# One more convolution tap per pair of query tiles, low parts of the first query weights on VectorE, and a reordered tail in a one-core mixer block

## The chip, the cores and the metric

The kernel runs on one core of one Trainium2 chip. The metric is the device time of one execution in microseconds (us), and what is compared is the median over several executions. A core has TensorE (PE in the profile) for matrix products, with its weight loads shown apart (PEld), VectorE (DVE), ScalarE (ACT), GpSimd (POOL), and SyncE (SP), which here only issues DMA transfers.

## The reference, cut to what matters

One layer of a hybrid block on 1024 latent tokens of width 1024, with 256 context tokens, all in float32:

```
h  = rms_norm(x, g_pre) * (1 + sc) + sh            # sh, sc, gt from silu(c) @ w_mod
hc = rms_norm(ctx, g_pre) * (1 + scc) + shc
ua, gate_a, q, k, v, gate_b, gm = split(h @ w_in)   # 7680 columns
k_c, v_c from hc @ w_in
q, k = rope(rms_norm(q)), rope(rms_norm(k));  k_c = rms_norm(k_c)
o = softmax(q @ [k, k_c].T / 8) @ [v, v_c]          # 16 heads, 4 kv heads, head size 64
y_attn = (o * silu(gate_b)) @ w_attn_out
y = a * sigmoid(g)                                  # ua = [a, g]
y = depthwise_conv(y, 31 taps) + conv_b
y_conv = (silu(layer_norm(y)) * silu(gate_a)) @ w_conv_out
out = (sigmoid(ga) * y_conv + sigmoid(gb) * y_attn) @ w_out      # gm = [ga, gb]
x_new = x + gt * rms_norm(out, g_post)
```

## The kernel before, in words

**Products.** Every large product is made of three matmuls in a reduced format: each operand is split into a high part (a copy that rounds, mostly on ScalarE) and a low part (operand minus high part, on VectorE or GpSimd), and the product is high·high + low·high + high·low. A *filler* is one such triple of 128x512 for one of the projections that only need `h` or the convolution's output (`ppj<-t,whi`, `ppj<-t,wlo`): the program spreads the fillers through the other stages to keep TensorE fed, by `filler(n)` and, in the context part, by the numbers that the generators yield (`yield 4` means: four fillers before this generator goes on).

**The stages**, with the times they have in the profiled execution. From 0 to 60 us `x` is loaded, modulated and transposed. From 60 to 143 us comes the context: `ctx_h` normalises and transposes the context tokens, `ctx_kv` makes their keys and values, and `group_w(0)` loads and splits the weights `wgh`, `wgl` of keys, values and queries of group 0. From 143 to 523 us the 16 pairs of (group `g`, query pair `q`): each has 48 matmuls `po<-wgh/wgl`, then `per` fillers. In between, `pump(n)` lets VectorE do `n` convolution taps (`pconv<-y,cw,pconv`, one multiply-add over 128x1024, with the sum kept in PSUM), `qkv_rope` turns queries and keys, and `qkv_tr` transposes them on TensorE two fillers into the next pair. The number `per` is what is left of a fixed supply of fillers, divided by 16: 21 here. From 523 to 575 us the rest of the projections, and the taps in `conv_rest` (the sum in SBUF there, `acc<-y,cw,acc`). From 575 to 1218 us the attention: scores `ps`, exponentials `pe` on ScalarE, row maxima `mx` of `pm` on VectorE, sums `part` and `psum` on VectorE and GpSimd, a filler for each step, and beside it the generators of `later`, which each go on after as many steps as they yield: the rest of the taps, `z_prep` (layer norm and gate of the convolution), `left_operands` and `right_operands`. The last two make and store the operands of the tail.

**The tail**, from 1249 us, does the two products with `w_attn_out` (side 0) and `w_out` (side 1) by seven block products each instead of eight, as in Strassen's scheme: `STEPS` has 14 steps of 48 matmuls. One factor of a step is a weight block or a sum of two, the other a block of the data or a sum of two: `O4` holds the four blocks of side 0's data (from `heads_load`), `M4` those of side 1. `data_sum` makes sums of blocks on GpSimd (`t<-t,t`), `data_split` makes the parts `opd`, `coef_load(i)` brings the weights of step `i`: as finished parts (`W<-opD`, `whi`, `wlo`) where attention stored them (the lists `LEFT` and `RIGHT`), else raw (`RAW`: load `raw`, high part on ScalarE, low part on GpSimd). `merge` (tiles `t`, `y`, `acc`) adds the block products of side 0 into `M4`; `finish` adds those of side 1, normalises and stores the result.

**What sets the order.** From the context part to the end of the 16 pairs, VectorE, ScalarE and GpSimd run in the order in which the code is written; each engine takes its instructions strictly one after the other, so one that waits holds up all that stand behind it on its engine. In the attention and the tail a scheduler places them by readiness and priority, and `urgent()` raises the priority of what is written inside.

## Time and profile before

| | |
|---|---|
| runs | 1427.43, 1432.18, 1434.3 us; median 1432.18 |
| profiled execution | 1428.95 us, of which the profile's span is 1427.2 |
| TensorE busy | 1362.0 us, 95% of the span |
| VectorE busy | 1084.9 us, 76% |
| GpSimd busy | 725.7 us, 51% |
| ScalarE busy | 565.4 us, 40% |
| granted TensorE clock, mean | 0.983 of full speed |

A share is an average over the stages; which engine sets the pace is read stage by stage. A line of a timeline gives the start, the duration, the engine and the operation, and in brackets how long the engine sat idle before it and who released it. A line of waits gives who waited for whom: the sum, how often, and the longest. All instructions are recorded by one helper at line 51 (`L51`), so the tile names tell them apart. Runs of equal instructions are merged into one line with `xcount`.

### The profile page before, as it was taken

To read this page: it belongs to the slowest core of one execution; us is meant where nothing else is said; L and a number is where in the kernel's file an instruction comes from. 1 tells how busy PE (TensorE), PEld (TensorE's weight loads), DVE (VectorE), ACT (ScalarE), POOL (GpSimd) and SP (SyncE) were. 2 spreads that over 40 slices of the span, in tenths; PEclk is the share of its full clock that TensorE was granted. 3 is DMA by queue.
4 is the path that set the end of the run, shared out by engine and by line. 5 is a ranking of instruction groups with operands and counts; after the bars stand their busy time and mean duration, and the time that the engine had idled before them with its cause. 6 is when DMAs were issued, how large, how long until landed. Compare 5 with 4: busy or idle time off the path is not lost.

```text
span 1427.2 us, 19268 instructions
## 1 busy us (share of the span) xinstructions
PE 1362.0 (95%) x6520; PEld 1037.9 (73%) x6520; DVE 1084.9 (76%) x1351; ACT 565.4 (40%) x1388; POOL 725.7 (51%) x567
## 2 busy tenths in 40 slices
PE   5989899999999999989999999999999999999896
PEld 3766788898989887757666676666666666788684
DVE  3486888988899899997577576677587675468977
ACT  5542234344343431224344355445354344122232
POOL 1122537557656550246467655666457676243722
PEclk9999999999999999989999999999999999999997
DMA  9733424445434437413246434654265567598653
GB/s 323 259 126 96 142 89 142 159 154 163 153 119 141 157 117 218 140 52 107 72 156 207 133 119 138 173 170 132 84 200 177 196 212 235 196 324 288 225 162 132
DMA packets 149762, 235.05 MB, mean 165 GB/s; under 512 B 19184, under 2 KB 71964, under 8 KB 149664
## 3 DMA queue, kind: packets, MB, share of 16 engines
q1 hardware_dynamic: 138784, 214.89, 45.9%
q10 hardware_dynamic: 10880, 18.95, 4.5%
q8 instruction: 51, 0.84, 0.2%
q14 instruction: 47, 0.39, 0.1%
HBM read 156.22 MB, written 77.42 MB: 164 GB/s over the span
## 4 chain that ended last, share of the span: by engine, by line
PE 72%; DVE 12%; DMA 4%; issue 4%; POOL 3%; ACT 3%; SPq 1%; ACTq 0%; POOLq 0%; DVEq 0%
PE ppj L51 32%; PE po L51 19%; PE ps L51 12%; PE pm L51 9%; DVE acc L51 3%; DVE t L51 2%; DVE mx L51 1%; DVE pconv L51 1%; POOL wgl L51 1%; DMA W<-opD 1%; DVE y L51 1%; POOL wlo L51 1%; DVE ts L51 1%; DVE opd L51 1%; DMA wm<-in_wmod 1%
## 5 line engine op out<-in xcount | busy, mean ns | idle before, releaser
L51 PE MATMUL ppj<-t,whi 128*128 128x512 f32 x1728 | 612.2, 398 | 5.0 <-DVE t L51 2.6
L51 PEld LDWEIGHTS ppj<-t,whi 128*128 128x128 f32 x1728 | 326.3, 189 | 91.7 <-issue 19.4
L51 PE MATMUL ppj<-t,wlo 128*128 128x512 f32 x864 | 339.0, 392 | 1.7 <-POOL wlo L51 1.7
L51 DVE TENSOR_REDUCE mx<-pm 128x1 f32<-128x512 f32 (+1 forms) x320 | 213.6, 682 | 94.0 <-PE pm L51 91.6
L51 ACT ACTIVATE pe<-ps 128x512 f32<-128x512 f32 x320 | 189.9, 598 | 220.1 <-PE ps L51 182.6
L51 PE MATMUL ps<-r,kk 128*128 128x512 f32 (+1 forms) x640 | 202.0, 397 | 5.6 <-ACT pe L51 5.6
L51 DVE SCALAR_TENSOR_TENSOR pconv<-y,cw,pconv 128x1020 f32<-128x1020 f32 (+14 forms) x157 | 200.8, 1279 | 6.9 <-ACT pconv L51 3.2
L51 POOL TENSOR_TENSOR psum<-psum,pe 128x512 f32<-128x512 f32 x128 | 189.3, 1495 | 28.1 <-ACT pe L51 25.3
L51 PEld LDWEIGHTS ppj<-t,wlo 128*128 128x128 f32 x864 | 163.4, 189 | 31.7 <-POOL wlo L51 2.1
L51 POOL TENSOR_TENSOR psum<-psum,part 128x512 f32<-128x512 f32 x64 | 90.7, 1421 | 113.3 <-DVE part L51 109.1
L51 PEld LDWEIGHTS ps<-r,kk 128*128 128x128 f32 (+1 forms) x640 | 120.1, 189 | 36.7 <-ACT pe L51 9.9
L51 PE MATMUL po<-pe,vt 128*64 128x512 f32 x640 | 144.4, 597 | 0.0
L51 PE MATMUL pm<-kk,r 128*128 128x512 f32 (+1 forms) x384 | 128.5, 363 | 6.9 <-DVE mx L51 6.6
L51 PE MATMUL po<-wgh,t 128*128 128x384 f32 x512 | 132.0, 339 | 0.0
L51 POOL TENSOR_TENSOR wlo<-wraw,whi 128x512 fp32r<-128x512 f32 x61 | 84.9, 1398 | 80.9 <-ACT whi L51 61.5
L51 DVE SCALAR_TENSOR_TENSOR acc<-y,cw,acc 128x1017 f32<-128x1017 f32 (+14 forms) x77 | 114.3, 1496 | 0.7
L51 PEld LDWEIGHTS po<-pe,vt 128*64 128x64 f32 x640 | 43.1, 136 | 84.8 <-issue 84.4
L51 PEld LDWEIGHTS po<-wgh,t 128*128 128x128 f32 x512 | 94.6, 191 | 1.3
L51 PEld LDWEIGHTS pm<-kk,r 128*128 128x128 f32 x384 | 73.1, 191 | 26.1 <-DVE mx L51 9.5
L51 PE MATMUL po<-wgl,t 128*128 128x384 f32 x256 | 87.4, 341 | 4.2 <-POOL wgl L51 4.1
L51 ACT CAST whi<-wraw 128x512 fp32r<-128x512 f32 x114 | 70.2, 633 | 39.4 <-PE ppj L51 23.2
L51 POOL TENSOR_TENSOR psum<-pe,pe 128x512 f32<-128x512 f32 x32 | 43.7, 1368 | 79.0 <-ACT pe L51 77.5
(210 smaller groups left out, 1854.2 us busy)
## 6 DMA issues: line engine op xcount, KB each, us to landing
wraw<-in_wch SPq DMA_DIRECT2D x96, 256.0 KB
opD<-opw SPq DMA_DIRECT2D x56, 256.0 KB
wm<-in_wmod SPq DMA_DIRECT2D x24, 512.0 KB
W<-opD SPq DMA_DIRECT2D x48, 256.0 KB
r1D<-r1st SPq DMA_DIRECT2D x32, 256.0 KB
y<-accD SPq DMA_DIRECT2D x16, 512.0 KB
r<-r1D ACTq DMA_DIRECT2D x32, 256.0 KB
opD<-acc SPq DMA_DIRECT2D x10, 512.0 KB
```

Source lines behind the costliest of these rows:

```text
L51: i = f(*a, **k)
```

## The change

It has eight parts:

1. More fillers in the context part: `ctx_h` yields 4 and 5 instead of 3 and 4, the last weights of `ctx_kv` 4 instead of 2, its end 8 instead of 6, `group_w(0)` 10 instead of 6. These are 10 more, and `per` becomes 20 (16 fewer in the 16 pairs; six go behind them).
2. One more tap per pair, at `i == 10`: 12 instead of 11 in each of the 16 pairs.
3. The low parts `wgl` of group 0 on VectorE instead of GpSimd.
4. `left_operands` yields 2 instead of 4.
5. `right_operands` makes five right operands per row block instead of four: block (1, 0), raw weights of `w_out`, is split and stored in the attention, and the tail loads its parts instead of splitting it (`RAW` loses its first entry).
6. `z_prep` takes 15 steps per channel block instead of 11.
7. `heads_load` loads its blocks in the order 0, 2, 1, 3, and `coef_load(0)` comes behind the first of them.
8. `data_sum` and `data_split` become urgent; `data_sum(0, 4, 3, SUB, 0)` moves from within the steps to before them; the sums of side 1 are made one step earlier, with a sixth entry of `M4`.

```
-        yield 3                       # ctx_h
+        yield 4
         scale()
-        yield 4
+        yield 5
...
-            yield 2                   # ctx_kv, after each split of weights
+            yield 2 if raw is not raws[-1] else 4
...
-        yield 6                       # ctx_kv, before the keys are transposed
+        yield 8
...
-        yield 6                       # group_w
+        yield 6 if g else 10
...
-            split(hi[:], lo[:], raws[k // 2][:], le=G)
+            split(hi[:], lo[:], raws[k // 2][:], le=G if g else V)
...
-    RIGHT = ((5, 0, (1, SUB, 0)), (7, 1, (3, SUB, 1)), (6, 3, (3, SUB, 0)), (4, 2, (2, SUB, 3)))
-    RAW = {(1, 1): lambda t: wout[t * P:(t + 1) * P, 0:512],
-           (1, 2): lambda t: wout[(t + 4) * P:(t + 5) * P, 0:512],
+    RIGHT = ((1, 0, None), (5, 0, (1, SUB, 0)), (7, 1, (3, SUB, 1)), (6, 3, (3, SUB, 0)), (4, 2, (2, SUB, 3)))
+    RAW = {(1, 2): lambda t: wout[(t + 4) * P:(t + 5) * P, 0:512],
...
-                yield 4               # left_operands
+                yield 2
...
-            for n in range(-1, 6):    # right_operands
+            for n in range(7):
                 if 2 <= n:
                     SP.dma_start(out=opD[1][RIGHT[n - 2][0]][t][:], in_=f32(w[n - 2][:]))
-                if 1 <= n <= 4:
+                if 1 <= n <= 5:
                     i = RIGHT[n - 1][1]
                     V.tensor_tensor(out=w[n - 1][:, 1, :], in0=b[i], in1=f32(w[n - 1][:, 0, :]), op=SUB)
...
-                if 0 <= n < 4:
-                    w[n] = tl("acc", (P, 2, 512), 2, F32R) if (4 * t + n) % 3 else tl("ysum", (P, 2, 512), 1, F32R)
+                if n < 5:
+                    w[n] = tl("acc", (P, 2, 512), 2, F32R) if (5 * t + n) % 3 else tl("ysum", (P, 2, 512), 1, F32R)
                     S.copy(w[n][:, 0, :], b[RIGHT[n][1]])
...
-        for b in range(4):            # heads_load
-            if b == 3:
+        for b in (0, 2, 1, 3):
+            if b in (2, 3):
                 yield
...
-    DATA = (0, 2, 4, 0, 3, 1, 2, 0, 4, 0, 1, 3, 4, 2)
+    DATA = (0, 2, 4, 0, 3, 1, 2, 0, 4, 5, 1, 3, 4, 2)
...
-            G.tensor_tensor(out=blk[to][t][:], in0=blk[a][t][:], in1=blk[b][t][:], op=op)
+            with urgent():
+                G.tensor_tensor(out=blk[to][t][:], in0=blk[a][t][:], in1=blk[b][t][:], op=op)
...
-            split(hi[:], lo[:], blk[t][:], le=le)
+            with urgent():
+                split(hi[:], lo[:], blk[t][:], le=le)
...
-                if i % 5 in (1, 3):
+                if i % 5 in (1, 3) or i == 10:
                     pump(1)
...
+        if i == 4:
+            data_sum(1, 5, 0, SUB, 1)
         if i == 5:
-            data_sum(1, 0, 0, SUB, 1)
-            data_sum(1, 4, 3, SUB, 0)
+            data_sum(1, 4, 3, SUB, 5)
```

**Group 0's weights.** The low parts `wgl` feed the first pair's matmuls; `wlo` is the same for the filler weights, `y` and `ts` are results of fillers that VectorE takes out of PSUM, `acc` a tap. In the kernel before, GpSimd's queue at the end of the context part reads:

```order
L51 TENSOR_TENSOR wlo_1266<-wraw_1222,whi_1265 128x512
L51 TENSOR_TENSOR wgl_1373<-wgr_1334,wgh_1372 128x768
L51 TENSOR_TENSOR wlo_1383<-wraw_1360,whi_1382 128x512
L51 TENSOR_TENSOR wgl_1393<-wgr_1337,wgh_1392 128x768
L51 TENSOR_TENSOR wlo_1400<-wraw_1362,whi_1399 128x512
L51 TENSOR_TENSOR wgl_1416<-wgr_1340,wgh_1415 128x768
L51 TENSOR_TENSOR wgl_1433<-wgr_1343,wgh_1432 128x768
```

In the changed kernel GpSimd has only the `wlo` there, and VectorE's queue reads:

```order
L51 SCALAR_TENSOR_TENSOR y_382_1213<-ts_1214,ppj_1323 128x512
L51 SCALAR_TENSOR_TENSOR acc_898<-y_313_839,cw,acc_898 128x1020
L51 TENSOR_TENSOR wgl_1416<-wgr_1361,wgh_1415 128x768
L51 SCALAR_TENSOR_TENSOR y_382_1213<-ts_1273,ppj_1401 128x512
L51 SCALAR_TENSOR_TENSOR acc_898<-y_313_839,cw,acc_898 128x1019
L51 TENSOR_TENSOR wgl_1434<-wgr_1364,wgh_1433 128x768
L51 TENSOR_TENSOR wgl_1459<-wgr_1367,wgh_1458 128x768
L51 SCALAR_TENSOR_TENSOR acc_898<-y_313_839,cw,acc_898 128x1018
L51 SCALAR_TENSOR_TENSOR ts_1479<-ts_1479,ppj_1441 128x512
L51 TENSOR_TENSOR wgl_1484<-wgr_1370,wgh_1483 128x768
```

The four `wgl` left a queue where they alternated with the `wlo` of the fillers, for one where two taps and three results of fillers stand among them.

**The start of the attention.** VectorE's queue in the kernel before, at the second pair of sums `part`:

```order
L51 TENSOR_TENSOR part_6223<-pe_6190,pe_6221 128x512
L51 TENSOR_REDUCE mx_6146<-pm_6226 128x1
L51 SCALAR_TENSOR_TENSOR acc_5594<-y_1073_5043,cw,acc_5594 128x1013
L51 TENSOR_REDUCE mx_6146<-pm_6242 128x1
L51 TENSOR_REDUCE mx_6146<-pm_6253 128x1
L51 SCALAR_TENSOR_TENSOR acc_5594<-y_1073_5043,cw,acc_5594 128x1012
L51 TENSOR_TENSOR wlo_6407<-wraw_6355,whi_6406 128x512
L51 TENSOR_REDUCE mx_6146<-pm_6286 128x1
```

And in the changed kernel at the same place:

```order
L51 TENSOR_TENSOR part_6238<-pe_6198,pe_6236 128x512
L51 TENSOR_REDUCE mx_6155<-pm_6256 128x1
L51 TENSOR_REDUCE mx_6155<-pm_6267 128x1
L51 TENSOR_TENSOR wlo_6422<-wraw_6368,whi_6421 128x512
L51 TENSOR_REDUCE mx_6155<-pm_6299 128x1
```

Of the 240 taps 21 stand behind the first row maximum of the kernel before, 15 of them behind the first `part`; in the changed kernel 5 and none.

**The sums of side 1.** GpSimd's queue in the tail of the kernel before (`t` are the blocks of `M4`, the first line a low part of a raw weight block):

```order
L51 TENSOR_TENSOR wlo_12527<-wraw_12528,whi_12526 128x512
L51 TENSOR_TENSOR t_2938_12047<-t_2938_12047,t_3010_12343 128x512
L51 TENSOR_TENSOR t_3065_12558<-t_3038_12455,t_2938_12047 128x512
L51 TENSOR_TENSOR wlo_12533<-wraw_12534,whi_12532 128x512
L51 TENSOR_TENSOR t_3010_12343<-t_3010_12343,t_3038_12455 128x512
L51 TENSOR_TENSOR t_2940_12064<-t_2940_12064,t_3012_12360 128x512
```

And in the changed kernel, where the last low parts of side 0's data (`opd<-O,opd`) stand:

```order
L51 TENSOR_TENSOR opd_12439<-O_2855_11687,opd_12438 128x512
L51 TENSOR_TENSOR t_3037_12446<-t_2942_12063,t_3014_12359 128x512
L51 TENSOR_TENSOR t_3038_12448<-t_2944_12080,t_3016_12376 128x512
L51 TENSOR_TENSOR t_3039_12450<-t_2946_12097,t_3018_12393 128x512
L51 TENSOR_TENSOR opd_12443<-O_2856_11688,opd_12442 128x512
L51 TENSOR_TENSOR t_3040_12452<-t_2948_12114,t_3020_12410 128x512
```

The four `wlo` of raw weights are gone, and the first difference of side 1 has moved ahead of the last `opd` of side 0.

## Rows read from the trace of the kernel before

**Rows 1.** The page, busy time, its share of the span, and instructions of each engine.

```profile
PE 1362.0 (95%) x6520; PEld 1037.9 (73%) x6520; DVE 1084.9 (76%) x1351; ACT 565.4 (40%) x1388; POOL 725.7 (51%) x567
```

**Rows 2.** Waits of TensorE, by what it waited for: us in total, times, longest. The stretches, parted by "...", are 60 to 165, 523 to 575, 575 to 720, 1240 to 1300 and 1300 to 1428 us.

```profile
PE po L51 <- POOL wgl L51: 4.1, 2, 3.6
PE po L51 <- DVE x L51: 2.1, 2, 1.3
PE pm L51 <- DVE ts L51: 1.8, 1, 1.8
PE ppj L51 <- POOL wlo L51: 1.7, 1, 1.7
PE ps L51 <- DVE x L51: 1.7, 2, 1.4
...
PE ppj L51 <- DVE ts L51: 2.4, 2, 1.4
PE pm L51 <- DVE qk L51: 1.7, 1, 1.7
...
PE pm L51 <- DVE mx L51: 6.8, 5, 4.4
...
PE ps L51 <- DMA W<-opD: 1.7, 1, 1.7
...
PE ps L51 <- DVE opd L51: 4.9, 2, 4.3
PE pm L51 <- DVE opd L51: 2.9, 2, 2.7
```

**Rows 3.** Stretches of the span: its length, busy us (and instructions) of each engine, granted TensorE clock, DMA share, GB/s.

```profile
142.97:159.10 16.13, 12.05 (x51) 10.92 (x50) 15.92 (x11) 1.29 (x12) 9.15 (x4) 0.79 0.45 145
...
173.34:500.00 326.66, 326.52 (x1636) 289.85 (x1636) 288.56 (x328) 134.62 (x575) 187.04 (x197) 1.00 0.43 142
...
626.00:630.00 4.00, 3.28 (x9) 2.07 (x9) 4.00 (x6) 0.60 (x1) 0.31 (x1) 0.50 0.00 0
630.00:634.00 4.00, 4.00 (x11) 3.17 (x12) 4.00 (x6) 0.87 (x2) 0.00 (x0) 0.52 0.00 1
...
1342.00:1346.00 4.00, 3.36 (x7) 2.25 (x8) 4.00 (x4) 0.00 (x0) 3.38 (x3) 0.50 0.55 166
```

**Rows 4.** Timeline at the first pair, 137 to 155 us: start, duration, engine, operation, in brackets the idle time before it and its releaser; ScalarE, GpSimd and TensorE one after the other.

```profile
137.67 0.83 ACT L51 CAST wgh<-wgr 128x768 fp32r<-128x768 f32 x1 [7.08 <-DMA wgr<-in_wq]
...
138.58 1.85 POOL L51 TENSOR_TENSOR wgl<-wgr,wgh 128x768 fp32r<-128x768 f32 x1 [15.15 <-ACT wgh L51]
146.60 5.53 POOL L51 TENSOR_TENSOR wgl<-wgr,wgh 128x768 fp32r<-128x768 f32 x2
...
137.78 0.39 PE L51 MATMUL ppj<-t,wlo 128*128 128x512 f32 x1
138.46 0.39 PE L51 MATMUL ppj<-t,wlo 128*128 128x512 f32 x1
143.32 0.34 PE L51 MATMUL po<-wgl,t 128*128 128x384 f32 x1
143.86 0.34 PE L51 MATMUL po<-wgl,t 128*128 128x384 f32 x1
```

**Rows 5.** Groups of VectorE's instructions with shape, count, busy us and mean ns, and idle time before them: taps with the sum in PSUM (whole span), low parts of filler weights in 523 to 575 us.

```profile
L51 DVE SCALAR_TENSOR_TENSOR pconv<-y,cw,pconv 128x1020 f32<-128x1020 f32 (+14 forms) x157 | 200.8, 1279 | 6.9 <-ACT pconv L51 3.2
...
L51 DVE TENSOR_TENSOR wlo<-wraw,whi 128x512 fp32r<-128x512 f32 x7 | 4.8, 684 | 0.6 <-ACT whi L51 0.5
```

**Rows 6.** Waits of VectorE in 173.34 to 500 us (14 pairs): us in total, times, longest.

```profile
DVE ts L51 <- ACT ts L51: 9.1, 5, 2.9
DVE kst L51 <- ACT kst L51: 4.1, 3, 2.2
DVE y L51 <- PE ppj L51: 3.6, 2, 3.3
```

**Rows 7.** Timeline of one pair: the last step of the rope on VectorE, and TensorE's first transposes of what it made.

```profile
389.07 1.25 DVE L51 TENSOR_TENSOR qk<-qk,qkt 128x640 f32<-128x640 f32 x1
...
394.20 0.82 PE L51 MATMUL pm<-ident,qk 128*64 128x128 f32 x6
```

**Rows 8.** Timeline of VectorE at the start of the attention: four taps with the sum in SBUF, which stand ahead of a row maximum.

```profile
616.24 8.95 DVE L51 SCALAR_TENSOR_TENSOR acc<-y,cw,acc 128x1022 f32<-128x1022 f32 x4
```

**Rows 9.** Groups in the attention (720 to 1218 us): high parts of right operands on ScalarE, with the idle time before them and who ended it.

```profile
L51 ACT CAST acc<-y 128x512 fp32r<-128x512 f32 x10 | 6.2, 621 | 17.7 <-POOL y L51 10.9 <-DMA opD<-acc 6.8
```

**Rows 10.** Timeline of SP's issues before the tail.

```profile
1239.63 2.36 SPq L1125 DMA_DIRECT2D O<-ogD  x5
...
1243.07 4.19 SPq L1141 DMA_DIRECT2D W<-opD  x6
```

**Rows 11.** Timeline of the tail, 1309 to 1342 us: GpSimd, then VectorE.

```profile
1309.06 3.55 POOL L51 TENSOR_TENSOR wlo<-raw,whi 128x512 fp32r<-128x512 f32 x2
1322.55 18.78 POOL L51 TENSOR_TENSOR t<-t,t 128x512 f32<-128x512 f32 x11
...
1319.07 0.68 DVE L51 SCALAR_TENSOR_TENSOR t<-acc,t 128x512 f32<-128x512 f32 x1
1340.13 1.75 DVE L51 TENSOR_TENSOR opd<-t,opd 128x512 fp32r<-128x512 f32 x1
```

**Rows 12.** Waits of VectorE at the end, 1374 to 1427 us: us in total, times, longest.

```profile
DVE q L51 <- ACT junk L51: 3.7, 7, 0.9
```

More of the change, by code (lines that the diff above doesn't have):

```diff
@@ L637, in right_operands @@
             w = {}
-            for n in range(-1, 6):
+            for n in range(7):
                 if 2 <= n:
                     SP.dma_start(out=opD[1][RIGHT[n - 2][0]][t][:], in_=f32(w[n - 2][:]))
-                if 1 <= n <= 4:
+                if 1 <= n <= 5:
                     i = RIGHT[n - 1][1]
                     V.tensor_tensor(out=w[n - 1][:, 1, :], in0=b[i], in1=f32(w[n - 1][:, 0, :]), op=SUB)
-                if n + 1 < 4:
-                    i, (x, op, y) = RIGHT[n + 1][1:]
-                    G.tensor_tensor(out=b[i], in0=b[x], in1=b[y], op=op)
-                if 0 <= n < 4:
-                    w[n] = tl("acc", (P, 2, 512), 2, F32R) if (4 * t + n) % 3 else tl("ysum", (P, 2, 512), 1, F32R)
+                for j in {0: (), 1: (1, 2)}.get(n, (n + 1,)):
+                    if j < 5:
+                        i, (x, op, y) = RIGHT[j][1:]
+                        G.tensor_tensor(out=b[i], in0=b[x], in1=b[y], op=op)
+                if n < 5:
+                    w[n] = tl("acc", (P, 2, 512), 2, F32R) if (5 * t + n) % 3 else tl("ysum", (P, 2, 512), 1, F32R)
                     S.copy(w[n][:, 0, :], b[RIGHT[n][1]])
-                yield 2 if n >= 0 else 1
+                if n < 6:
+                    yield 2
     R1 = {}
@@ L1040, in z_prep @@
             SP.dma_start(out=g[:], in_=gaD[j][:])
-            yield 2
+            yield 3
             if j + 1 < KD:
                 load(j + 1)
-            yield 2
+            yield 3
             for tok in HALVES:
@@ L1047, in z_prep @@
                 yield 1
+            yield 1
             th = tl("ysum", (P, T), 1)
@@ L1051, in z_prep @@
             G.tensor_tensor(out=a[j][:], in0=a[j][:], in1=g[:], op=ALU.mult)
-            yield 2
+            yield 3
             for tok in HALVES:
@@ L1114, in block_kernel @@
     O4 = []
-    M4 = [[None] * 4 for _ in range(5)]
+    M4 = [[None] * 4 for _ in range(6)]
     data, coef, tmp, gates = {}, {}, {}, {}
@@ L1149, in data_sum @@
         for t in range(4):
-            if to == 4 != b:
-                blk[4][t] = tl("t2", (P, 512), 32)
-            G.tensor_tensor(out=blk[to][t][:], in0=blk[a][t][:], in1=blk[b][t][:], op=op)
+            if to > 3 and to != b:
+                blk[to][t] = tl("t2", (P, 512), 32)
+            with urgent():
+                G.tensor_tensor(out=blk[to][t][:], in0=blk[a][t][:], in1=blk[b][t][:], op=op)
     def data_split(i, le=V):
@@ L1158, in data_split @@
             hi, lo = tl("opd", (P, 512), 16, F32R, "C"), tl("opd", (P, 512), 16, F32R, "C")
-            split(hi[:], lo[:], blk[t][:], le=le)
+            with urgent():
+                split(hi[:], lo[:], blk[t][:], le=le)
             data[i].append((hi, lo))
     def data_ready(i):
-        if i == 2:
-            data_sum(0, 4, 3, SUB, 0)
         if i == 3:
@@ L1472, in block_kernel @@
     coef_load(0)
+    next(heads)
     filler(12)
@@ L1482, in block_kernel @@
     O4.append([None] * 4)
+    data_sum(0, 4, 3, SUB, 0)
     for t in range(4):
```

## The prediction

> **What bounds the kernel now.** I read the page first: TensorE is busy for 1362.0 of 1427.2 us [rows 1]. The change takes no matmul away, so all that it can win lies in the 65 us in which TensorE stands still, and in stretches where it works at half its clock. The second view is therefore TensorE's waits by stretch [rows 2]. The reader should see that they are few and each has an owner: 11.4 us up to the first pair of query tiles, 4.1 us behind the 16 pairs, 6.8 us at the start of the attention, 1.7 us before the tail, 7.8 us in it. The third view, busy time and clock by stretch [rows 3], shows two things. In the 14 pairs from 173 to 500 us TensorE is busy for 326.52 of 326.66 us: there is nothing to win in them. And after a wait of several us the granted clock is at 1.2 instead of 2.4 GHz for some us (0.50 and 0.52 of full speed from 626 to 634 us, 0.50 from 1342 to 1346 us), so that a long wait costs more than its own length.
>
> **Context and first pair.** A filler takes 138.46 − 137.78 = 0.68 us [rows 4]. Three matmuls `po` take 143.86 − 143.32 = 0.54 us, so the 48 of a pair take 16 x 0.54 = 8.6 us; the first pair's took about 16.1 us (51 matmuls in that stretch), at a mean clock of 0.79 [rows 3, 4]. The 7.5 us too much are the 4.1 us of waits for `wgl` [rows 2] and the clock behind them. The cause is GpSimd's queue: ScalarE's first `wgh` came late, after a wait of 7.08 us for its load, and from then GpSimd makes low parts of 1.85 us, at the end of 5.53/2 = 2.8 us each, with the `wlo` between them, until 146.60 + 5.53 = 152.1 us [rows 4]. The change gives four more fillers (2.7 us) between the loads and the first pair, and moves the four low parts to VectorE. The trace has no `wgl` there. The lower bound is 0.684 us for 128x512 with a quiet GpSimd [rows 5], times 768/512: 1.03 us. The upper is 1.75 us for 128x512 with a busy one [rows 11]: 2.6 us. I take the lower, since only the `wlo` are left on GpSimd. Four of 1.03, with the two taps (1.28 each [rows 5]) and three results of fillers (0.7 each) between them, are 8.8 us from 138.5 us on: until 147.3. TensorE comes to the pair at about 144 and to its last quarter 6.5 us later, at 150.5: covered by 3 us. At the upper price the last comes at 153.6, 3 us late, and with the clock behind it 6 us come back.
>
> At the four other waits one or two fillers more (0.7 to 1.4 us) stand ahead of what waits: 2.1 and 1.7 us for `x`, 1.8 us for `ts` [rows 2]; I count 1.4, 1.5 and 1.6. The 1.7 us for `wlo`, which stands behind a `wgl` in GpSimd's queue, go. With 7.5 that is 13.7; less some rest of waits, **−12** (bounds −6 and −14). The fillers themselves are moved, not added: 10 earlier and 6 later for 16 fewer in the pairs, which costs nothing where TensorE is the bound.
>
> **The 16 pairs.** A pair takes 326.66/14 = 23.33 us, and with one filler less 22.65. VectorE is busy for 288.56/14 = 20.61 us of it [rows 3]. Of its 38.1 idle us, 9.1 + 4.1 + 3.6 = 16.8 are waits for results that would lie ready if VectorE were late [rows 6]; the rest I count as part of its chain: (326.66 − 16.8)/14 = 22.13 us a pair. One more tap, 1.28 us [rows 5], makes 23.4: VectorE falls behind by 0.75 us a pair. It has a reserve: in the pair shown its rope ends at 389.07 + 1.25 = 390.3 us, and the first transposes of it start at 394.20 [rows 7]: 3.9 us, five pairs' worth. After that, by this bound, it sets the pace for eleven pairs: +8. By the other bound all its idle time can be filled (20.61 + 1.28 = 21.9 < 22.65): 0. I take +4, in the middle, since it is near neither. Behind the pairs stand 2.4 + 1.7 us of waits for `ts` and `qk` [rows 2], which the taps of the last pair cause; that pair has fewer taps now, but a later VectorE: I count −1. Together **+3** (bounds −3 and +8).
>
> **Start of the attention.** The 16 more taps before it leave 5 behind the first row maximum instead of 21, and none behind the first `part` instead of 15. Four of these took 8.95 us, 2.2 us each [rows 8], and the row maximum behind them gave the wait of 4.4 us among the 6.8 [rows 2]; from 626 to 634 us TensorE then worked at 1.2 GHz, which lost about 3.5 us more [rows 3]. That is 10.3; I take **−9** (bounds −6, if the scheduler puts the row maxima behind other work, and −10).
>
> **Attention.** Four more high parts on ScalarE (0.621 us each), which wait in its queue for GpSimd's sums and for stores, 17.7 us for ten [rows 9]; what is queued behind them are the exponentials, and TensorE's scores wait for those. `z_prep` is only spread. Bounds: 0, if they fall into ScalarE's idle time as most do now, and 4 x (0.6 + 1.8) = 10. I take **+1**, near the lower.
>
> **Tail.** The weights of step 0 stand behind eleven loads `O` in SP's queue (the last five and the weights: [rows 10]) and cost 1.7 us [rows 2]; with seven of those behind them: **−1.7**. The wait of 4.3 us for `opd` at 1342 us [rows 2] comes from VectorE's queue, which runs its three-tile work at 1.75 us a piece instead of 0.68 while GpSimd makes eleven sums in a row for 18.78 us [rows 11]. The change takes four `wlo` of 1.8 us off GpSimd [rows 11] and makes the first difference earlier, so the sums end some 7 us earlier and VectorE's last pieces run at the fast price. With the 0.6 us behind it and the half clock to 1346 us [rows 2, 3] the stall is worth 6.9 us; I take **−5.5** (bounds 0 and −7). The waits of 2.9 us at the end [rows 2] are worth less than they look, for there VectorE goes step by step with ScalarE (3.7 us of waits in seven pieces [rows 12]), and that chain ends the kernel: **−1** (bounds 0 and −3).
>
> By a rule of the Trainium skill (SBUF — State Buffer, section "Who interferes with whom"), a VectorE instruction with two SBUF inputs and a GpSimd instruction that reads SBUF shut each other out: the one that issues second waits for the whole of the first. The trace agrees in kind (0.68 and 1.75 us for pieces of one size, [rows 11]). By it the `wgl` on VectorE would pay the upper price whenever a `wlo` runs on GpSimd; the sum would be −19 instead of −25.
>
> **Sum.** −12 + 3 − 9 + 1 − 1.7 − 5.5 − 1 = −25.2 us. The profiled execution took 1428.95 us, so 1403.7 for one like it. It lies 3.2 us below the median of its runs, 1432.18; half of that I give to the median of the changed kernel, and round up: **1406 us**. The bounds of the terms together are −39 and +4; all ends on one side are unlikely.
>
> **Rivals.**
> - *The low parts on VectorE come late.* At 2.6 us a piece the first pair stalls again for 3 us, and with the clock 6 us come back: 1411–1412.
> - *VectorE becomes the bound in the pairs.* For it speaks the 23.4 against 22.65 us; against it the idle time that may be filled. It gives +8 in the pairs and another 4 to 5 us behind them, since VectorE then enters the rest of the taps late and the keys of the last pair with it: 1406 + 10 = 1416.
> - *The waits come back behind the next engine* in the attention and the tail: TensorE comes earlier to the next row maximum or part that is not ready. Then only the context and the first weights count, −12 + 3 + 1 − 1.7 = −9.7: 1421.
> - *Slower: ScalarE's queue in the attention.* Twenty high parts instead of sixteen share the same three buffers, and each must wait until its predecessor's store has landed; exponentials queue behind it. If each of the 20 holds TensorE for 2 us, with the clock behind every second one, that is 40 us and more: 1406 + 38 = 1444. It decides the sign from 25 us on, that is from 1.25 us for each of the twenty. Against it: the sixteen of now wait 1.8 us each on an engine that is busy for 40% [rows 1, 9].
>
> **How the numbers follow.** About 0.5%, 7 us, is what a measurement of this kernel can tell from no change: faster is below 1425, slower above 1439. The forecast has 0.47 (its own range 1397 to 1413), the late low parts 0.10, VectorE as the bound 0.17, the waits that come back 0.12, the slow attention 0.14. Of these, 0.02 of the third, 0.04 of the fourth and 0.04 of the fifth fall within 0.5%, 0.10 of the fifth beyond: faster 0.80, same 0.10, slower 0.10. The range 1395 to 1428 leaves out most of the fifth and what lies below the forecast.
>
> **What would show it.** Right: no wait for `wgl` and a first pair of about 8.6 us for its 48 matmuls; pairs of 22.65 us with TensorE busy throughout; no wait above 1 us for `mx` between 600 and 640 us (on the old time axis) and no half clock there; first matmuls of the tail without a wait for `W`; no 4 us wait for `opd` in side 1's first steps. Wrong: pairs longer than 22.8 us with TensorE waiting for `qk` (VectorE is the bound); TensorE waiting for `pe` by more than 10 us in the attention (ScalarE's queue); a granted clock of 0.5 where it is 1.00 now.

## The result: faster by a third of what was forecast

The changed kernel takes 1421.96 us (median of 10 runs, 1417.45 to 1426.28) against 1429.55 us for the kernel before (10 runs); the ratio is 0.9943, 95% interval 0.9924 to 0.9962. That is 8 us or 0.6% faster. The forecast was 1406 us, 26 us faster than the median then known; its range, 1395 to 1428, holds the result. The profiled execution of the changed kernel has a span of 1420.6 us against 1427.2.

TensorE's waits in the changed kernel (us in total, times, longest), which answer to [rows 2]. The stretches, parted by "...", are 60 to 165, 165 to 523, 523 to 575, 575 to 720, 720 to 1218, 1218 to 1300 and 1300 to 1428 us; sums of 0.5 us or less are left out:

```profile
PE ppj L51 <- DVE y L51: 3.2, 2, 3.0
PE pm L51 <- DMA wm<-in_wmod: 1.0, 2, 0.7
PE po L51 <- DVE x L51: 1.0, 1, 1.0
...
PE ppj L51 <- DVE ts L51: 3.4, 4, 1.5
PE pm L51 <- DVE qk L51: 2.9, 4, 2.0
PE ppj L51 <- DVE y L51: 2.0, 2, 1.3
...
PE ppj L51 <- DVE y L51: 1.9, 1, 1.9
PE ppj L51 <- DVE ts L51: 1.4, 2, 0.8
...
PE pm L51 <- DVE mx L51: 2.5, 3, 1.8
PE ppj L51 <- DVE ts L51: 1.3, 1, 1.3
...
PE ps L51 <- ACT pe L51: 6.4, 7, 1.5
...
PE pm L51 <- DMA whi<-opD: 2.1, 1, 2.1
...
PE ps L51 <- DVE opd L51: 0.9, 1, 0.9
```

The reader should see both halves. The waits that the prediction counted are gone or small: none for `wgl`, `wlo` and `W`, 2.5 us for `mx` instead of 6.8, 0.9 for `opd` instead of 7.8 in two lines. And there are new ones: 3.0 us for `y` in the context, 2.1 us for `whi` in the tail, and 8.3 us in the 16 pairs, where the kernel before had none.

The stretches show the same: the first pair's 48 matmuls (with three more), the 14 pairs behind it, and the start of the attention (columns as in [rows 3]).

```profile
149.10:157.80 8.70, 8.70 (x51) 8.64 (x50) 8.56 (x9) 1.38 (x13) 0.00 (x0) 1.00 0.73 221
171.14:502.50 331.36, 322.48 (x1597) 282.77 (x1597) 306.25 (x343) 134.64 (x580) 188.36 (x199) 0.99 0.44 141
604.30:676.10 71.80, 71.08 (x323) 48.82 (x323) 48.28 (x63) 32.32 (x57) 42.09 (x29) 1.00 0.27 86
```

The first pair takes 8.7 us instead of 16.1 and has its clock throughout; the 14 pairs, from which 14 fillers (9.5 us) were taken, take 331.4 us instead of 326.7; at the start of the attention TensorE is busy for 71.1 of 71.8 us.

**Where the time went.** Waits alone leave out what a low clock costs. So I took, for each stage, the time that it lasted less the number of TensorE's matmuls of each kind in it times their usual spacing in the kernel before. What is left I call lost time. It does not change when fillers move. In the attention its level means little, since the spacing there is itself set by other engines; only differences between kernels count. Executions of the same code differ by up to 4 us in the context and by about 3 us in other stages, so that smaller differences are no evidence by themselves. The first two rows of the table are best read as one: in the two other runs with the old code of this stretch (experiments 3 and 13) the context lost 2.5 and 3.8 us more than in the profile of the kernel before, and the first pair 2.7 and 2.8 us less. Together they came to −8.1 us where −12 was forecast.

```
us lost            before  after  change  forecast
context             33.4   32.8    -0.6     -4.5   (with the end of the first loads)
first pair           7.6    0.1    -7.5     -7.5
other 15 pairs       1.9   15.4   +13.5     +4
to the attention     7.1    9.4    +2.3     -1
start of attention  24.0   16.3    -7.7     -9
rest of attention  150.2  150.9    +0.7     +1
to the tail          6.8    5.0    -1.8     -1.7
tail, steps 0, 1     0.5    4.4    +3.9      0
tail, steps 7, 8     7.6    1.3    -6.3     -5.5
tail, steps 9 to 13  6.8    0.0    -6.9  }  -1
behind the matmuls  11.1   14.9    +3.8  }
sum                                -6.6
```

Five of the stages came as forecast or nearly; the 16 pairs, the stretch behind them, the context and a new wait in the tail's second step took the rest back.

### The profile page after: what moved, and what is told of

Its sections match the earlier page's. It is cut to its first block, busy times and chain, and to the rows that moved or that the text cites. A ratio compares the mean times of both kernels' runs of the same rounds, so it can differ in the third digit from the quotient of the medians.

```text
span 1420.6 us, 19284 instructions
## 1 busy us (share of the span) xinstructions
PE 1359.5 (96%) x6520; PEld 1033.5 (73%) x6520; DVE 1072.7 (76%) x1359; ACT 565.0 (40%) x1388; POOL 705.2 (50%) x559
## 4 chain that ended last, share of the span: by engine, by line
PE 55%; DVE 20%; issue 10%; DMA 5%; POOL 5%; ACT 3%; SPq 1%; ACTq 0%; POOLq 0%; DVEq 0%
PE ppj L51 21%; PE po L51 15%; PE ps L51 11%; PE pm L51 8%; DVE pconv L51 7%; DVE acc L51 2%; DVE t L51 2%; DVE qk L51 2%; POOL wlo L51 1%; DVE qkt L51 1%; DVE r1st L51 1%; DVE ts L51 1%; DVE y L51 1%; DMA wraw<-in_wch 1%; POOL y L51 1%
## 5 line engine op out<-in xcount | busy, mean ns | idle before, releaser
L51 PE MATMUL ppj<-t,whi 128*128 128x512 f32 x1728 | 617.0, 399 | 16.1 <-DVE y L51 7.0
L51 DVE SCALAR_TENSOR_TENSOR pconv<-y,cw,pconv 128x1012 f32<-128x1012 f32 (+14 forms) x174 | 222.5, 1279 | 10.0 <-ACT pconv L51 5.7
L51 POOL TENSOR_TENSOR psum<-psum,pe 128x512 f32<-128x512 f32 x128 | 184.8, 1458 | 27.7 <-ACT pe L51 24.3
L51 PEld LDWEIGHTS ps<-r,kk 128*128 128x128 f32 (+1 forms) x640 | 120.0, 189 | 38.5 <-ACT pe L51 11.8
L51 DVE SCALAR_TENSOR_TENSOR acc<-y,cw,acc 128x1009 f32<-128x1009 f32 (+14 forms) x60 | 80.3, 1339 | 2.3 <-ACT acc L51 1.3
```

Source lines behind the costliest of these rows:

```text
L51: i = f(*a, **k)
```

## The experiments

Each edit is against the changed kernel unless it says otherwise; the kernel before had medians of 1427.9 to 1429.5 us beside them. Ratios are to it; the changed kernel's is 0.9943.

**1. The extra tap undone.** (`z_prep` has its old yields, without which it does not end in time.)

```
-                if i % 5 in (1, 3) or i == 10:
+                if i % 5 in (1, 3):
```

> The changed kernel without its extra tap in the 16 pairs (11 taps each again) and with z_prep's old yields, which it then needs to end in time; all else as changed. My theory: the extra tap is what makes VectorE the bound in the pairs. Then TensorE's waits from 165 to 523 us fall from 9.0 to under 2 us and the lost time there by 12 us; in return the row maxima at the start of the attention wait again (6.8 us and half clock behind them, 8 us): about 1418 us against 1422 for the changed kernel. Rival: the pairs are slow because they are one filler shorter and GpSimd's left operands, made faster now, slow VectorE down; then the waits in the pairs stay above 5 us and the whole takes about 1429 us.

Measured: 1430.6 us, ratio 1.0009 (0.9995 to 1.0023). The waits of TensorE in the pairs:

```profile
PE pm L51 <- DVE qk L51: 1.8, 2, 1.3
PE ppj L51 <- DVE ts L51: 1.1, 1, 1.1
PE ppj L51 <- DVE y L51: 0.3, 1, 0.3
PE ppj L51 <- ACT ts L51: 0.3, 1, 0.3
```

The pairs lost 6.9 us instead of 15.4: the tap costs them 8.5, as my theory had it in kind, but 5 us of loss remain over the kernel before. What is left to explain them is the shorter pair (20 fillers) with the new yields of `left_operands` that go with it: this generator runs in the pairs, one step behind each filler (its `opw` are made from 175 to 528 us in the changed kernel), not in the attention as the description of the stages says. The time is not what the theory gave: the start of the attention lost 5.1 us more, the rest of it 7.5 more and the stage ahead 4.0. So the 16 taps are dearer behind the pairs than in them, by more than the first wait of the attention that I had priced; how much of the 7.5 us belongs to the old yields of `z_prep` is not shown.

**2. The extra tap in half of the pairs.**

```
+                if i % 5 in (1, 3) or i == 10 and q % 2:
```

> The changed kernel with the extra tap in every second pair only (8 more instead of 16). My theory, from VectorE's work per pair: 22.13 + 0.64 = 22.8 us against 22.65 of TensorE, so that it falls behind by 1 us over all pairs, within its reserve: waits of TensorE in the pairs below 3 us instead of 9.0, and 13 taps behind the first row maximum, few of them behind the first part: about 1412 us. Rival (each tap costs the same wherever it stands): the waits in the pairs halve, to 4 to 5 us, and half of the 8 us at the start of the attention come back: 1420 us.

Measured: 1424.73 us, ratio 0.9968 (0.9952 to 0.9984). The pairs lost 11.5 us, between 6.9 and 15.4, as the rival said: the cost goes with the number of taps, there is no reserve within which a few are free. The stage behind the pairs lost 16.5 us instead of 9.4; the code makes there, in one go, what is left of a channel's taps, and how many those are depends on the count before. That this is the cause was not shown.

**3. The extra tap alone, in the kernel before** (21 fillers per pair).

```
-                if i % 5 in (1, 3):
+                if i % 5 in (1, 3) or i == 10:
```

> The kernel before with the extra tap per pair alone. By my theory the pairs, at 23.33 us, lose less than 4 us, and the start of the attention gains the 8 us that it gained in the changed kernel: about 1424 us against 1429 before. By the rival (the tap makes VectorE the bound at 23.33 us too) the pairs lose 10 us or more and the time is 1431 us or above.

Measured: 1433.11 us, ratio 1.0024 (1.0005 to 1.0042): slower than before. The theory falls: with a pair of 23.33 us the pairs lost 11.8 us against 1.9. The start of the attention won 8.2 us, as in the changed kernel, and the stage ahead of it lost 5.5. TensorE's waits in 165 to 523 us, and the stretch of the pairs:

```profile
PE ppj L51 <- POOL wlo L51: 2.3, 1, 2.3
PE po L51 <- ACT qk L51: 1.8, 1, 1.8
PE ppj L51 <- DVE y L51: 1.7, 2, 1.1
PE pm L51 <- DVE qk L51: 0.5, 1, 0.5
```

```profile
172.90:510.20 337.30, 330.86 (x1640) 291.08 (x1639) 304.52 (x342) 133.93 (x575) 187.51 (x197) 0.99 0.42 138
```

VectorE is busy for 304.5 of 337.3 us, 90%; over the whole stretch it isn't full. And only 2.2 of the 6.3 us of waits are for VectorE itself. Before the wait for `wlo`, GpSimd had made a sum `ysum` of 2.40 us at 230.87 us, which in the kernel before came at 241.64 us, behind that `wlo`: one more tap per pair also shifts the end of each channel of the convolution, and with it work of other engines. That this shift makes the wait was not tested apart.

**4. 21 fillers again, the rest as changed** (the old yields in the context part and in `left_operands`).

```
-        yield 6 if g else 10
+        yield 6
...
-                yield 2
+                yield 4
```

> The changed kernel with the old yields of the context part and of left_operands, so that a pair has 21 fillers again; the extra tap, the low parts on VectorE and the tail as changed. My theory now: TensorE can't bear a VectorE that is late by 1.5 us, since it waits for results of fillers that VectorE takes out of PSUM in the order of its queue; a pair of 22.65 us is too short for VectorE with 11 or 12 taps, one of 23.33 us holds both. Then the lost time in the pairs falls from 15 to under 4 us, the waits for x and ts in the context come back (5 us), the first pair stays without a wait for wgl: about 1414 us. Rival: twelve taps (23.4 us by the prediction's bound) are too many at 23.33 us too; then 10 us are lost in the pairs and the whole takes 1421 us.

Measured: 1424.58 us, ratio 0.9959 (0.9944 to 0.9974). The pairs lost 10.3 us instead of 15.4, the context 3.9 more, the stage ahead of the attention 5.0 more; in sum the same. The rival was right: twelve taps are too many for 23.33 us too, and the shorter pair, with the yields of `left_operands`, costs 5 us more. In the context the waits for `x` and `ts` are back (5.6 us), but the wait for `y` at its end did not go with the added fillers; it is longer, in 60 to 165 us:

```profile
PE ppj L51 <- DVE y L51: 5.8, 1, 5.8
```

**5. to 7. The same tap at other places.** VectorE's work per pair is that of the changed kernel in all three: the extra tap leaves its place behind filler 11 for one of these.

```
-            pump(3)                                        # among the matmuls po
+            pump(4)
...
-                if i % 5 in (1, 3) or i == 10:
+                if i % 5 in (1, 3) or i == 4:              # behind the fifth filler
...
+                if i % 5 in (1, 3) or i == per - 1:        # behind the last filler
```

> The changed kernel with the extra tap of a pair moved: from between fillers 10 and 11 into the matmuls po of the pair, where three taps stand already and no filler's result waits for VectorE. VectorE's work per pair is the same. Theory (latency: what TensorE waits for are results of fillers that stand behind taps in VectorE's queue): the lost time in the pairs falls from 15 us to 11 or less, and the whole is 4 us faster than the changed kernel. Rival (VectorE's sum of work per pair decides): the lost time in the pairs stays at 13 to 17 us, the time at 1422 us.

> The changed kernel with the extra tap behind the fifth filler of a pair. In the trace of before VectorE's idle time lies in the middle of a pair (fillers 2 to 8). Theory (place): the lost time in the pairs falls below 12 us. Rival (any tap ahead of filler 10 delays the results behind it, as among the matmuls po, where 24 us were lost): more than 15 us are lost, the time is 1425 us or above.

> The changed kernel with the extra tap of a pair behind its last filler instead of behind the eleventh. The same work of VectorE per pair. Theory (place: a tap costs what it delays; in the changed kernel VectorE's queue is full from filler 10 on, and TensorE waits there, while behind the last filler come 8 us of matmuls po without a filler's result): lost time in the pairs 8 us or less against 15, the whole about 1415 us. Rival: the delay only moves to the rope, which stands next in VectorE's queue, and to the transposes that wait for it: lost time of 15 us or more, waits for qk instead of ts, 1422 us or above.

Measured: among the matmuls 1431.86 us (ratio 1.0020, 1.0004 to 1.0037), behind the fifth filler 1432.53 (1.0022, 1.0007 to 1.0038), behind the last 1426.09 (0.9979, 0.9966 to 0.9991). The pairs lost 23.9, 22.3 and 19.7 us, against 15.4 with the tap behind filler 11. The largest waits in 165 to 523 us, first with the tap among the matmuls, then behind the last filler:

```profile
PE ppj L51 <- DVE ts L51: 7.6, 5, 2.7
PE ppj L51 <- DVE y L51: 4.4, 2, 2.6
PE ppj L51 <- ACT ts L51: 3.1, 3, 1.2
PE pm L51 <- DVE qk L51: 0.9, 2, 0.7
```

```profile
PE pm L51 <- DVE qk L51: 7.7, 5, 2.7
PE ppj L51 <- DVE ts L51: 2.9, 2, 1.5
PE ppj L51 <- DVE y L51: 2.7, 2, 1.5
```

The work is the same and the loss differs by 8.5 us, so VectorE's sum per pair does not decide alone. The owner of the wait follows the tap: put ahead of the fillers, it delays their results (`ts`, `y`); put at the end, it delays the rope (`qk`); behind the fifth filler it delays both (7.2 us for `ts` and `y`, 4.8 for `qk`). But no place was free, and my guess at a better one was wrong three times: the changed kernel has the best of the four.

**8. Loads of group 0's weights earlier.**

```
-        yield 8                # end of ctx_kv
+        yield 6
...
-        yield 6 if g else 10   # group_w
+        yield 6 if g else 12
```

> The changed kernel with two of the fillers moved from before to behind the loads of group 0's weights (the end of ctx_kv yields 6 as before, group_w(0) 12). My theory: the wait of 3.0 us for y at 141 us and the half clock behind it come from those loads, which stand in SP's queue behind two loads of filler weights that wait for GpSimd; ScalarE's first wgh waits 10.2 us for them, VectorE's first wgl for that, and y stands behind it. Then the wait shrinks below 1 us and the time falls by 4 to 5 us, to about 1417 us. Rival: the loads of filler weights only move behind it and the wait goes to wlo or wgl at the first pair: 1422 us.

Measured: 1423.89 us, ratio 0.9955 (0.9938 to 0.9973): no gain. The wait for `y` fell from 3.0 to 2.1 us, a new one of 0.7 us for `ts` came, and the tail's second step lost 1.5 us more. Nothing of 4 us shows in the sum. The two loads of filler weights still stand ahead of those of group 0 in this run (issued at 132.23 and 135.80 us), so it did not take away what it was aimed at.

**9. The first low part back on GpSimd.**

```
-            split(hi[:], lo[:], raws[k // 2][:], le=G if g else V)
+            split(hi[:], lo[:], raws[k // 2][:], le=V if g == 0 and k else G)
```

> The changed kernel with the first of group 0's four low parts back on GpSimd, the other three on VectorE. Theory (the wait of 3.0 us for y at 141 us is y standing behind that low part in VectorE's queue, which waits for ScalarE's wgh and that for its load): the wait for y and the half clock behind it go, 4 to 5 us, with no new wait for wgl: 1417 us. Rival: a wait of the same size for wgl, wlo or ts follows within the next 10 us: 1422 us.

Measured: 1422.06 us, ratio 0.9950 (0.9931 to 0.9970): as the rival said. The chain at the end of the context in the changed kernel is this (ScalarE, GpSimd, VectorE, TensorE, then SP's issues):

```profile
142.18 0.83 ACT L51 CAST wgh<-wgr 128x768 fp32r<-128x768 f32 x1 [10.24 <-DMA wgr<-in_wq]
...
131.49 4.71 POOL L51 TENSOR_TENSOR wlo<-wraw,whi 128x512 fp32r<-128x512 f32 x2 [8.46 <-ACT whi L51]
145.36 3.53 POOL L51 TENSOR_TENSOR wlo<-wraw,whi 128x512 fp32r<-128x512 f32 x2 [9.15 <-ACT whi L51]
...
143.05 0.96 DVE L51 TENSOR_TENSOR wgl<-wgr,wgh 128x768 fp32r<-128x768 f32 x1 [5.76 <-ACT wgh L51]
143.92 0.68 DVE L51 SCALAR_TENSOR_TENSOR y<-ts,ppj 128x512 f32<-128x512 f32 x1
145.71 3.99 DVE L51 TENSOR_TENSOR wgl<-wgr,wgh 128x768 fp32r<-128x768 f32 x2
...
144.66 0.50 PE L51 MATMUL ppj<-t,whi 128*128 128x512 f32 x1 [3.02 <-DVE y L51]
...
134.01 2.55 SPq L146 DMA_DIRECT2D wraw<-in_wch  x2
137.57 0.42 SPq L581 DMA_DIRECT2D wgr<-in_wkv  x1
```

TensorE waits for `y`, which stands behind `wgl` in VectorE's queue; that waits for ScalarE's `wgh`, that for its load, and the load stood in SP's queue behind two loads of filler weights, which wait for GpSimd's `wlo`. Those two loads are not what makes the wait: in experiment 4 they don't stand there, and `y` waits 5.8 us. With the first `wgl` on GpSimd the `y` is free (0.2 us), and TensorE comes to the first pair 4.6 us earlier (144.5 instead of 149.1 us), where the weights are still missing:

```profile
PE po L51 <- DVE wgl L51: 2.8, 2, 2.4
PE po L51 <- DVE x L51: 1.0, 1, 1.0
PE po L51 <- POOL wgl L51: 0.9, 1, 0.9
```

The first pair then loses 6.2 us instead of 0.1, the context 4.8 less.

**10. and 11. The loads before the tail.** The changed kernel's old order of the heads' loads, and, apart from it, urgent loads for step 1.

```
-        for b in (0, 2, 1, 3):
-            if b in (2, 3):
+        for b in range(4):
+            if b == 3:
```

```
-    coef_load(1)
+    with urgent():
+        coef_load(1)
```

> The changed kernel with the old order of the heads' loads. If the order only moved a wait from step 0 (1.8 us for W) to step 1 (3.9 us for whi with the clock behind it), the old order is faster by 2 us: 1420 us. If the wait for whi has another cause (more loads in the tail), W waits again on top of it: 1424 us.

> The changed kernel with the loads of step 1's weights (whi, wlo) made urgent. My theory: the wait of 2.1 us for whi at 1259 us and the half clock behind it (3.9 us in all) come from the twelve loads of O that now stand in SP's queue between W and whi; with whi ahead of them the time falls by 3 to 4 us, to about 1418 us. Rival: the buffers of whi come free only with the last fillers, so that the loads can't start earlier and nothing changes, or an O block becomes late instead: 1422 us.

Measured: old order 1421.18 us (ratio 0.9934, 0.9911 to 0.9957), urgent loads 1424.5 us (0.9957, 0.9940 to 0.9975). SP's issues in the changed kernel, and TensorE's matmul behind them:

```profile
1240.48 2.35 SPq L1143 DMA_DIRECT2D W<-opD  x5
1243.86 3.51 SPq L1127 DMA_DIRECT2D O<-ogD  x6
1251.42 2.83 SPq L1127 DMA_DIRECT2D O<-ogD  x6
1254.35 0.65 SPq L1143 DMA_DIRECT2D whi<-opD  x1
...
1261.10 0.47 PE L51 MATMUL pm<-opd,whi 128*128 128x512 f32 x1 [2.09 <-DMA whi<-opD]
```

Twelve loads of `O` stand between `W` and `whi` now, where the old order has four. With the old order, TensorE's only wait in 1218 to 1300 us is this one for `W`, and steps 0 and 1 lose 1.1 us instead of 4.4:

```profile
PE ps L51 <- DMA W<-opD: 0.7, 2, 0.4
```

The median moved by 0.8 us, less than its interval, so the 3 us of the trace are shown there only. In the two other kernels with the old order (experiments 14 and 15) `W` waits 1.4 and 1.9 us again, so that the way to the tail and steps 0 and 1 together lost 8.7 and 7.5 us there, 6.5 here, 9.4 in the changed kernel and 7.3 in the kernel before. Urgent loads take the wait for `whi` away and put one of 3.8 us for a result `t` of ScalarE at the start of step 2: the rival's "something else becomes late".

**12. Four right operands instead of five.** (`RIGHT`, `RAW` and the loop of `right_operands` as before.)

> The changed kernel with four right operands instead of five, so that the tail splits four raw weight blocks on ScalarE and GpSimd again. If GpSimd's relief is what took the 4.3 us wait for opd out of side 1's first steps, as the prediction has it, a wait of 3 us or more for opd returns there and the time rises by 5 us, to 1427 us. Rival: the urgent sums and their earlier place alone do it; no wait above 1 us in the tail's steps 7 and 8, and the attention is faster by a few us without the fifth operand: 1418 us.

Measured: 1421.46 us, ratio 0.9939 (0.9916 to 0.9962). Both theories were half right. TensorE's waits in 1218 to 1428 us:

```profile
PE ps L51 <- DVE opd L51: 3.2, 4, 1.3
PE pm L51 <- DMA whi<-opD: 2.3, 1, 2.3
```

Without the fifth operand steps 7 and 8 lose 6.7 us again (1.3 with it, 7.6 before), though the sums are urgent and early; so GpSimd's relief is what that term rests on. And the attention loses 142.8 us instead of 150.9. What the fifth operand wins in the tail it costs ahead of it.

**13. The tail's parts alone, in the kernel before** (fifth operand, order of loads, urgent sums, sixth block).

> The kernel before with the parts for the tail alone: the fifth right operand, the order of the heads' loads, the urgent sums and splits with the sixth block. The tail's terms as read from the changed kernel: 6.3 us for the wait for opd, 3 us at the end, 1.8 us before the tail, 3.9 us lost to the wait for whi: 1422 us against 1429. Rival (the tail's gain needs the earlier attention of the changed kernel, or the five operands cost the attention what the tail gains): 1429 us.

Measured: 1425.01 us, ratio 0.9968 (0.9953 to 0.9983): faster by 4.6 us. The tail's stages came as in the changed kernel (steps 7 and 8: 1.3 us lost, steps 9 to 13: none), so its gain does not need the rest; 3.3 us more were lost in the attention.

**14. and 15. Combinations.** First old order, tap among the matmuls, first low part on GpSimd; then old order and four operands.

> The changed kernel with three edits: the old order of the heads' loads, the extra tap among the matmuls po, and the first low part of group 0 on GpSimd. By the theories of the three, 2 + 4 + 4 us less than the changed kernel: 1412 us. If the first alone holds, 1420 us.

> The changed kernel with four right operands and the old order of the heads' loads, the two parts whose undoing cost nothing each (1421.5 and 1421.2 us). If their effects add as the traces say (8.1 us less lost in the attention, 5.4 more in the tail's steps 7 and 8, 3.3 less in step 0 and 1): 6 us less than the changed kernel, 1416 us, a ratio of about 0.990 to the kernel before. If the old order's gain needs the fifth operand's loads out of the way or the attention's gain is only a shift between executions: 1421 us.

Measured: 1429.23 us (1.0008, 0.9992 to 1.0023) and 1417.68 us (0.9920, 0.9895 to 0.9946). The first has the tap's wrong place and shows its price again (23.3 us lost in the pairs). The second has the lowest median of all kernels here, but its interval overlaps that of the changed kernel, and in its profile the attention lost 148.1 us, not 142.8: how much of the 8 us belongs to the fifth operand stays open, between 3 and 8.

## Why the prediction was right in sign and wrong in size

- **Context (−4.5 forecast for `x` and `ts`, −0.6 measured).** The waits for `x` and `ts` shrank from 5.6 us to 1.0 as forecast, and without the added fillers they are back (experiment 4). What the forecast lacks is the wait of 3.0 us for `y` and the clock behind it. The step that failed is the move of `wgl` to VectorE: the prediction named the taps and results between the `wgl`, but asked only whether the `wgl` would be late, not what is late behind them. VectorE's first `wgl` waits 5.76 us for `wgh` and so for its load, and `y` stands behind it; with this `wgl` on GpSimd the wait for `y` is 0.2 us (experiment 9). The load came 4.5 us later than before (142.18 against 137.67 us [rows 4]), in part behind two loads of the added fillers' weights, but without these the wait is 5.8 us (experiment 4).
- **First pair (−7.5 forecast and measured).** One `wgl` alone took 0.96 us on VectorE, a little less than the lower bound, two in a row 3.99 while GpSimd made two `wlo` (experiment 9), which is 2.0 each and between the bounds; no wait for `wgl` came of it. With the Trainium skill's rule (SBUF — State Buffer, "Who interferes with whom") that pieces of the two engines shut each other out the trace agrees here, 0.96 us apart and 2.0 us beside GpSimd; the loss that the rule would have meant for the first pair did not come.
- **The pairs (+4 forecast, bounds 0 and +8; +13.5 measured).** This is the term that the result hangs on. Two steps failed: the reserve, and VectorE's mean over a pair as the measure. The reserve, "3.9 us, five pairs' worth", was read in one pair, and from the rope alone [rows 7]. In another pair of the same trace the last step of the rope, which takes 2.91 us there beside a sum `ysum` on GpSimd, ends 0.3 us before the transposes of what it made:

```profile
437.71 2.91 DVE L51 TENSOR_TENSOR qk<-qk,qkt 128x640 f32<-128x640 f32 x1
...
440.91 0.82 PE L51 MATMUL pm<-ident,qk 128*64 128x128 f32 x6
```

The results of fillers were not asked for at all, and 5.4 of the 8.3 us of waits in the changed kernel's pairs are for them (`ts`, `y`), 2.9 for the rope. And the choice of the middle between two bounds because "it is near neither" had no row behind it; the rival with VectorE as the bound, at 1416 us, was closer than the forecast. And the mean does not measure the loss. Without a reserve the prediction's bound gives 0.75 x 16 = 12 us, near what came, and that is luck: the same bound gives 1 us for twelve taps in 23.33 us, where experiment 3 lost 9.9 more than the kernel before, and nothing for eleven taps in 22.65 us, where experiment 1 lost 5.0 more. Shown: the tap costs 8.5 to 9.9 us in the pairs at either length, the shorter pair with its yields of `left_operands` 5, the place of the tap up to 8.5 more.

- **Behind the pairs (−1 forecast, +2.3 measured).** The waits of before for `ts` and `qk` gave way to others for `y` and `ts`. The stage lost from 7.1 to 16.5 us as the taps per pair changed (experiments 1 to 4); why was not shown.
- **Start of the attention (−9 forecast, −7.7 measured).** Right, and in experiment 3 with the tap alone too (−8.2).
- **Attention (+1 forecast, +0.7 measured).** The number is right by a sum of two effects: fewer taps give time (experiment 3: 5.9 us less lost than before), the fifth operand takes it (experiments 12 and 13: 3 to 8 us). The step that put the fifth operand near 0, because its work falls "into ScalarE's idle time as most do now", was too low; the slower kernel by ScalarE's queue, the rival on the other side, did not come, but its mechanism fits the 3 to 8 us. That ScalarE's queue is the cause was not shown.
- **Before the tail (−1.7 forecast, −1.8 measured) and step 1 (0, +3.9).** The step that moves loads of `O` behind `W` asked only about `W`; the queue's next customer, `whi`, took over the wait, larger.
- **Tail (−5.5 forecast, −6.3 measured).** Right, and by the cause named: experiment 12 brings the loss back when GpSimd gets its four `wlo` again.
- **End (−1 forecast, −3.1 measured).** The lost 6.9 us in TensorE's last steps went entirely; 3.8 of them came back behind the last matmul, in VectorE's chain with ScalarE, as the prediction said it would, only less. Since these 6.9 us stay away with four operands too, they belong to the urgent sums and splits and the sixth block, which no run takes apart.

What stays open is why the extra tap is worth 9 us inside the changed kernel (experiment 1, with `z_prep` changed too) and costs 4 alone (experiment 3). In the lost time nearly all of the difference is the stage ahead of the attention, which with the tap loses 4.0 us less in the one and 5.5 us more in the other.

## What to carry to other kernels

When work is added to an engine that is busy for nine tenths of a loop, ask which of its results has the least time to spare, and in which turn of the loop, not how much of its time is free: a reserve of 3.9 us in one pair was 0.3 us in another, and TensorE waited for results of fillers and for the rope while VectorE was idle for 8 to 10% of the loop. An instruction moved to another engine's queue holds up what stands behind it there: the `wgl` were not late on VectorE, but `y` behind them was. A reordered queue moves a wait to its next customer: follow the queue to its end before counting the gain.

## What the runs showed of the hardware that was not expected

A wait of 3 us for `y` was followed by a stretch at the lower clock level of TensorE, and so was one of 2.1 us for `whi`; columns as in [rows 3]:

```profile
145.00:149.00 4.00, 4.00 (x12) 3.12 (x11) 4.00 (x3) 2.85 (x5) 3.53 (x2) 0.58 0.52 164
...
1260.00:1264.00 4.00, 2.79 (x7) 2.04 (x8) 1.10 (x1) 1.10 (x2) 4.00 (x4) 0.72 1.05 403
```

The granted clock averaged 0.58 and 0.72 there. An estimate for the first: 3.0 us of wait and 42% of the 4 us behind it are 4.7 us. For the second the table of lost time has 3.9 us more in steps 0 and 1, with a wait of 2.1 us. Where a wait only moved, the low clock came behind its new place: in experiment 9 the first pair lost 6.2 us with 3.7 us of waits for `wgl`, and the granted clock averaged 0.55 from 153 to 155 us.
